# One layer of a hybrid decoder on one core: weight columns streamed in two interleaved halves, and segment sums kept in PSUM

## The chip, the cores and the metric

The kernel runs on one core of a Trainium2 chip. The metric is the device time of one execution in microseconds (us). Before the change the median of three runs is 2433.56 us (2433.44 to 2435.43).

## The reference, cut to what matters

Input is a float32 matrix of 256 tokens by 2048 features. The layer is an FFN, a two-branch mixer and a second FFN, each followed by a layer norm.

```
swiglu(h, w_in, w_out):  a, b = split(h @ w_in, 2);  return (silu(a) * b) @ w_out     # 2048 -> 2 x 5632 -> 2048
h = layer_norm(ALPHA*h + 0.5*swiglu(h, ffn1_w_in, ffn1_w_out))
q, k, v, qi, ki, wi, rx, rg, gates = split(h @ w_in)
y_attn = indexer-selected sparse attention(q, k, v, qi, ki, wi)
y_rnn  = gated linear recurrence(rx, rg)
merged = g_attn * (y_attn @ w_attn_branch) + g_rnn * (y_rnn @ w_rnn_branch)
h = layer_norm(ALPHA*h + merged @ w_out)
h = layer_norm(ALPHA*h + 0.5*swiglu(h, ffn2_w_in, ffn2_w_out))
```

## The kernel before, in words

**Products.** Every float32 operand is split into a high and a low part of the type fp32r: ScalarE rounds (`wh`, line 192), VectorE subtracts (`wl`, line 193). A product is then three matmuls, high by high, high by low and low by high. There are two kinds. In the *token-major* products the activations are the stationary operand (128 tokens at a time) and the weights stream past, 512 or 256 columns in one matmul; they all go through `three` (lines 553 to 556) and write 128 tokens by 512 columns of output. They are the two FFNs, the attention projections (`blockA`) and the product with `w_out`. In the others (`blockB`, `block3`) the weights are stationary and the activations stream; these are not touched by the change.

**Weights.** `Weights` walks a fixed list of pieces of 128 by 1024. A piece is loaded from HBM by SyncE's queue, split by ScalarE and VectorE four pieces ahead of TensorE, and consumed by `unit`. There are five buffers each of `wh` and `wl`.

**The FFN.** The 5632 hidden features are worked off in 22 blocks of 256 (a block holds 256 columns of each half of `w_in`). In most blocks three quarters of the sum over the 2048 features ("chunks") use a scheme with seven instead of eight 128x256 products for two-by-two tiles (forms `p1q3`, `p2`, `q5p7`, `q4p6`), with sums that VectorE forms beforehand (lines 165 to 172); the last quarter is plain ("c"). A block's result lies in two PSUM banks `c` and two banks `e`; `gate` (lines 842 to 871) joins them, applies the gate and transposes.

**The second product of the FFN** is spread over the blocks. The 22 blocks form six segments, `SEGS`, of 2, 4, 4, 4, 4 and 4 blocks. While a segment is worked off, the product of the segment before it with its rows of `w_out` runs as *fills* ("o" in a block's plan), for one 512-column stripe `nb` of the output after the other. Blocks 2 to 5 have two fills each, blocks 6 to 21 have four ("steady blocks" below): two at the start of the block, one after three forms, one after nine, and then three more forms. So each block from 2 on completes one stripe of one segment: two PSUM banks, one for each half of the tokens. `y_add` (line 689) then adds 0.5 times each bank to the running sum `Y[t][nb]` in SBUF; this is one VectorE instruction for each half. The last segment's product comes after the blocks (`out_product`).

**PSUM.** Eight banks: four under the tag `mm` (handed out in turn by `MM` to the `c` banks, to the fills, and to the products of the mixer), four under `bp`.

**Order.** TensorE, SyncE and GpSimd issue in the order in which the program is written. The instructions of ScalarE and VectorE are put in order by the scheduler of the language when the program is built.

Of the kernel before, what the change touches and what calls it, by code (L numbers as in the profile page):

```python
# [261 lines left out]
def tile_layer(ctx, tc, x_fm, x_tm, pos, f1a, f1o, wA, wki, wB, lru, wab, wrb, wo, f2a, f2o,  # L262
# [24 lines left out]
    def C(shape, s, dt=F32):  # L287
        return pool.tile(shape, dt, name=s)

    def MM():  # L290
        return psum.tile([P, 512], F32, name=name("mm"), tag="mm", bufs=4)

    def BP():
        return psum.tile([P, 512], F32, name=name("bp"), tag="bp", bufs=4)
# [255 lines left out]
            mmB(ps, x[k], W.unit(P), k == 0, k == len(x) - 1)  # L550
        return ps

    def three(ps, xh, xl, w, start, stop):
        T.matmul(ps, xh, w[0], start=start, stop=False)  # L554
        T.matmul(ps, xh, w[1], start=False, stop=False)  # L555
        T.matmul(ps, xl, w[0], start=False, stop=stop)  # L556

    def tokens(ps, x, t, w, start, stop):
        three(ps, x[:, 0, t * P:(t + 1) * P], x[:, 1, t * P:(t + 1) * P], w, start, stop)

    def eager(x, ps):

# [16 lines left out]
    def blockF(x, forms, plan, fill):  # L579

        c = e = None

        seen = set()
        last = {f: i for i, (f, k) in enumerate(plan)}
        top = max(last["c"], last.get("p2", 0)), max(last["c"], last.get("q4p6", 0))
        skip = 0
        if getattr(x, "halves", None):
            c = [MM(), MM()]  # L590
            eager(x, c)
            skip = 4
        for i, (form, k) in enumerate(plan):
            if i < skip:
                continue
            if form == "o":
                fill()
                continue
            if form == "c":
                if not c:  # L600
                    c = [MM(), MM()]
                    half = [c[0][:, :S], c[0][:, S:], c[1][:, :S]]
                for k in range(k, k + 2):
                    w = W.unit(512)
                    for t in range(2):
                        tokens(c[t], x[k], t, w, k == 0, k % 2 == 1 and i == top[t])
                continue
            if not e:
                e = [BP(), BP()]
                p1, p6, p7, q5 = e[0][:, :S], e[0][:, S:], e[1][:, :S], e[1][:, S:]  # L610
            start = form not in seen
            seen.add(form)
            stop = i == last[form]
            fs = [forms[2 * k + r] for r in range(2)]

            def xop(r, i, t):
                v = x[4 * k + 2 * r + i]
                return v[:, 0, t * P:(t + 1) * P], v[:, 1, t * P:(t + 1) * P]

            def sop(r, i):  # L620
                return tuple(v[:, i * P:(i + 1) * P] for v in fs[r])

            def run(ps, op, start, stop):
                for r in range(2):
                    three(ps, *op(r), W.unit(S), start and r == 0, stop and r == 1)

            if form == "p1q3":
                run(p1, lambda r: xop(r, 0, 0), start, False)
                run(half[1], lambda r: sop(r, 3), False, False)
            elif form == "p2":  # L630
                run(half[0], lambda r: xop(r, 1, 0), False, i == top[0])
            elif form == "q5p7":
                run(q5, lambda r: sop(r, 0), start, False)
                run(p7, lambda r: sop(r, 2), False, stop)
            else:
                run(half[2], lambda r: xop(r, 1, 1), False, i == top[1])
                run(p6, lambda r: sop(r, 1), False, stop)
        return c, e
# [202 lines left out]
    def ffn(x, forms, ln, plans):  # L841
        def gate(c, e, g, i, lag):

            z = W.fast_pool.tile([P, 4 * S], F32, name=name("z"), tag="z", bufs=Z_BUFS)
            z4 = z.rearrange("p (j c) -> p j c", j=4)
            a, b = z4[:, 0:4:2], z4[:, 1:4:2]
            if e:
                p1, p6, p7, q5 = e[0][:, :S], e[0][:, S:], e[1][:, :S], e[1][:, S:]
                A.activation(z4[:, 0], p1, AF.Copy)
                V.tensor_tensor(z4[:, 1], z4[:, 0], p6, op=OP.add)  # L850
                V.tensor_tensor(z4[:, 2], z4[:, 1], p7, op=OP.add)
                V.tensor_tensor(b, q5[:, None, :].to_broadcast([P, 2, S]), z4[:, 1:3], op=OP.subtract)
                for t in range(2):
                    zt = z[:, t * 512:(t + 1) * 512]
                    V.tensor_tensor(zt, zt, c[t], op=OP.add)  # L855
                A.activation(a, a, AF.Silu)
            else:
                for t in range(2):
                    A.activation(z4[:, 2 * t], c[t][:, :S], AF.Silu)
                    A.activation(z4[:, 2 * t + 1], c[t][:, S:], AF.Copy)  # L860
            V.tensor_tensor(a, a, b, op=OP.mult)
            for _ in range(lag):
                yield
            ps = BP()
            for k in range(2):
                for t in range(2):
                    T.transpose(ps[:, k * S + t * P:k * S + (t + 1) * P], z[:, t * 512 + k * P:t * 512 + (k + 1) * P], ident)  # L867
            for k in range(2):
                hl = UHL("g")
                split(hl, ps[:, k * S:(k + 1) * S])  # L870
                g[i + k] = hl

        g = [[None] * (2 * (b1 - b0)) for b0, b1 in SEGS]
        fills = iter(FILLS)
        open_ps = []

        def fill():
            s, nb, k0 = next(fills)
            if k0 == 0:
                open_ps[:] = MM(), MM()  # L880
            for k in (k0, k0 + 1):
                w = W.unit(512)
                for t in range(2):
                    tokens(open_ps[t], g[s][k], t, w, k == 0, k == len(g[s]) - 1)
            if k0 + 2 == len(g[s]):
                for t in range(2):
                    y_add(open_ps, nb, False, t)

        for s, (b0, b1) in enumerate(SEGS):
            for n in range(b0, b1):  # L890
                c, e = blockF(x, forms, plans[n], fill)
                task = gate(c, e, g[s], 2 * (n - b0), LAG_T[n == NBK - 1])
                next(task)
                bg.add("gate", task)
        new_stats()
        ln.prepare()
        if not ln.last:
            bg.add("main", later(consts(), W.last.ins))
        out_product(g[-1], ln)
# [306 lines left out]
def _layout(x, positions, ffn1_w_in, ffn1_w_out, ln1_g, ln1_b, w_in, conv_w, conv_b, lru_wa, lru_ba,  # L1206
# [5 lines left out]
        return np.ascontiguousarray(a)  # L1212

    def f_in(w):
        return c(w.reshape(NK, P, 2, NBK, 256).transpose(3, 1, 0, 2, 4)).reshape(NBK, P, NK * 512)

    def f_out(w):
        return c(w.reshape(NKF, P, 4, 512).transpose(2, 1, 0, 3)).reshape(4, P, NKF * 512)

    def a_blocks(w):  # L1220
        n = w.shape[1] // 512
        return c(w.reshape(NK, P, n, 512).transpose(2, 1, 0, 3)).reshape(n, P, NK * 512)

    def b_blocks(w):
        nk, n = w.shape[0] // P, w.shape[1] // P
# [52 lines left out]
```

## Time and profile before

| what | value |
|---|---|
| median of three runs | 2433.56 us |
| span of the profiled execution, and its own time | 2433.4 us |
| TensorE busy | 2400.1 us (99%) |
| VectorE busy | 2041.4 us (84%) |
| ScalarE busy | 1413.4 us (58%) |
| DMA, mean over the span | 190 GB/s |
| mean granted clock of TensorE | 0.996 of 2.4 GHz |

Read it so: TensorE has matmuls under way at nearly all times, but that says nothing of the rate at which they run. That has to be read from the distance between the starts of neighbouring matmuls. VectorE's 84% is a mean over stages: in the FFNs it is far higher than in the mixer. The first FFN takes about the first 695 us, the mixer lies between, and the second FFN begins shortly after 1700 us.

### The profile page before, as it was taken

The page shows a single profiled execution, that of the slowest core. Times are in us where ns is not written, and L with a number is a line of the kernel's source. Part 1 is how long each engine was busy: PE and PEld are TensorE (multiplying, and loading weights), DVE is VectorE, ACT ScalarE, POOL GpSimd, SP SyncE. Part 2 cuts the span into 40 slices and gives each one's busy share as a digit, 9 for nine tenths or more (in the row PEclk, how much of TensorE's full clock was granted, in tenths as well). Part 3 has the DMA queues.
Part 4 walks back from the last instruction along what each step waited for, and adds up shares of the span by engine and source line. Part 5 has one row for each costly group of instructions (what it writes and reads, how often), then busy time and mean ns, then how long its engine had stood idle before and what let it go on. Part 6 is the DMA issues. An engine that isn't in the chain of part 4 may idle for free.

```text
span 2433.4 us, 37546 instructions
## 1 busy us (share of the span) xinstructions
PE 2400.1 (99%) x14592; PEld 2117.5 (87%) x14592; DVE 2041.4 (84%) x2835; ACT 1413.4 (58%) x1931; POOL 25.9 (1%) x58
## 2 busy tenths in 40 slices
PE   8999999999999999999999999999999999999997
PEld 7888889888878788889999988887888888888885
DVE  8999999999987676555788875655999999999996
ACT  7555556656546455544688874444665555565562
POOL 0000000000000000000000000000000000000001
PEclk9999999999999999999999999999999999999998
DMA  8545555555456554455555565565655555555563
GB/s 291 187 176 188 208 208 208 205 187 205 183 165 216 166 164 147 152 186 184 181 185 188 181 197 184 188 186 181 209 206 195 203 195 187 186 188 218 208 212 113
DMA packets 112770, 463.41 MB, mean 190 GB/s; under 512 B 12720, under 2 KB 12720, under 8 KB 97488
## 3 DMA queue, kind: packets, MB, share of 16 engines
q1 hardware_dynamic: 110592, 454.61, 54.5%
q0 software_dynamic: 2000, 6.41, 1.0%
q8 instruction: 114, 1.87, 0.3%
q14 instruction: 64, 0.52, 0.1%
HBM read 458.87 MB, written 2.10 MB: 189 GB/s over the span
## 4 chain that ended last, share of the span: by engine, by line
PE 91%; issue 4%; DVE 3%; DMA 1%; ACT 1%; POOL 0%; SPq 0%; DVEq 0%; ACTq 0%; POOLq 0%
PE mm L554 16%; PE mm L556 16%; PE mm L555 16%; PE mm L544 11%; PE mm L545 5%; PE bp L556 4%; PE bp L555 4%; PE bp L554 4%; PE mm L1129 4%; PE mm L1130 4%; PE mm L1128 4%; DVE wl L193 2%; PE bp L867 1%; DMA raw<-f1a 0%; DVE ws L165 0%
## 5 line engine op out<-in xcount | busy, mean ns | idle before, releaser
L193 DVE TENSOR_TENSOR wl<-raw,wh 128x1024 fp32r<-128x1024 f32 (+3 forms) x630 | 753.1, 1203 | 290.2 <-ACT wh L192 289.0
L192 ACT ACTIVATE wh<-raw 128x1024 fp32r<-128x1024 f32 (+3 forms) x630 | 653.8, 1046 | 550.5 <-PE mm L556 290.6
L192 ACT ACTIVATE wh<-rf 128x1024 fp32r<-128x1024 f32 x354 | 321.0, 917 | 172.2 <-PE mm L556 138.4
L193 DVE TENSOR_TENSOR wl<-rf,wh 128x1024 fp32r<-128x1024 f32 x354 | 366.8, 1043 | 5.5 <-ACT wh L192 2.6
L554 PE MATMUL mm<-wh,g 128*128 128x512 f32 x704 | 282.2, 401 | 2.0 <-ACT g L679 2.0
L556 PE MATMUL mm<-wh,g 128*128 128x512 f32 x704 | 279.7, 397 | 1.3 <-DVE g L680 1.3
L555 PE MATMUL mm<-wl,g 128*128 128x512 f32 x704 | 279.0, 396 | 0.0
L554 PE MATMUL mm<-wh,hs 128*128 128x512 f32 (+1 forms) x728 | 265.4, 365 | 1.9 <-DVE z L855 1.9
L556 PE MATMUL mm<-wh,hs 128*128 128x512 f32 (+1 forms) x728 | 261.2, 359 | 1.1 <-DVE hs L745 1.1
L555 PE MATMUL mm<-wl,hs 128*128 128x512 f32 (+1 forms) x728 | 260.6, 358 | 0.0
L192 ACT ACTIVATE wh<-ws 128x1024 fp32r<-128x1024 f32 x118 | 125.3, 1062 | 163.8 <-issue 70.4
L556 PE MATMUL bp<-wh,sl 128*128 128x256 f32 x708 | 198.0, 280 | 0.0
L554 PE MATMUL bp<-wh,sh 128*128 128x256 f32 x708 | 197.6, 279 | 0.0
L555 PE MATMUL bp<-wl,sh 128*128 128x256 f32 x708 | 197.5, 279 | 0.0
L544 PE MATMUL mm<-hs,wh 128*128 128x512 f32 x528 | 190.1, 402 | 0.0
L1128 PE MATMUL mm<-hs,wh 128*128 128x256 f32 x640 | 179.8, 281 | 0.0
L1130 PE MATMUL mm<-hs,wl 128*128 128x256 f32 x640 | 179.8, 281 | 0.0
L1129 PE MATMUL mm<-hs,wh 128*128 128x256 f32 x640 | 179.8, 281 | 0.0
L554 PE MATMUL mm<-wh,xs 128*128 128x256 f32 (+1 forms) x464 | 158.5, 342 | 8.5 <-ACT wh L192 6.2
L556 PEld LDWEIGHTS mm<-wh,g 128*128 128x128 f32 x704 | 132.7, 189 | 34.6 <-DVE g L680 2.5
L193 DVE TENSOR_TENSOR wl<-ws,wh 128x1024 fp32r<-128x1024 f32 x118 | 144.5, 1224 | 19.8 <-ACT wh L192 19.8
L554 PEld LDWEIGHTS mm<-wh,hs 128*128 128x128 f32 x728 | 136.6, 188 | 28.0 <-issue 4.3
(255 smaller groups left out, 5347.8 us busy)
## 6 DMA issues: line engine op xcount, KB each, us to landing
raw<-wB SPq DMA_DIRECT2D x144, 512.0 KB, 3.8
rf<-f1a SPq DMA_DIRECT2D x60, 1024.0 KB, 4.8
rf<-f2a SPq DMA_DIRECT2D x58, 1024.0 KB, 5.0
raw<-f1o SPq DMA_DIRECT2D x88, 512.0 KB, 5.7
raw<-f2o SPq DMA_DIRECT2D x88, 512.0 KB, 5.9
raw<-wA SPq DMA_DIRECT2D x64, 512.0 KB, 3.6
raw<-f2a SPq DMA_DIRECT2D x60, 512.0 KB, 4.9
raw<-f1a SPq DMA_DIRECT2D x56, 512.0 KB, 5.8
```

The source lines that it names most:

```text
L192: nc.scalar.activation(hp, src, AF.Copy)
L193: self.last = nc.vector.tensor_tensor(lp, src, hp, op=OP.subtract)
L544: T.matmul(ps, w[0], x.rearrange("p a t -> p (a t)"), start=first, stop=False)
L545: T.matmul(ps[:, :S], w[1], x[:, 0], start=False, stop=last)
L554: T.matmul(ps, xh, w[0], start=start, stop=False)
L555: T.matmul(ps, xh, w[1], start=False, stop=False)
L556: T.matmul(ps, xl, w[0], start=False, stop=stop)
L867: T.transpose(ps[:, k * S + t * P:k * S + (t + 1) * P], z[:, t * 512 + k * P:t * 512 + (k + 1) * P], ident)
L1128: T.matmul(ps[:, :S], w[0], x[:, 0], start=first, stop=False)
L1129: T.matmul(ps[:, :S], w[0], x[:, 1], start=False, stop=False)
L1130: T.matmul(ps[:, :S], w[1], x[:, 0], start=False, stop=last)
```

## The change

It has two parts. In the first, `three` hands its two weight operands to the matmul through another view: of each 256 columns as they lie in SBUF, the matmul now takes column 0, column 128, column 1, column 129 and so on, that is, two runs of addresses 512 bytes apart, in alternation. The weights are laid out in HBM on the host so that the outputs stand in the same order as before. Loads, splits and sums see tiles of the same shape.

In the second, the PSUM tag `mm` becomes two tags of two banks each: `CB` (still named `mm`) for the `c` banks, `OB` (`ob`) for the fills; the other users take one and the other in turn. For segments 1 to 4 of each FFN (the steady blocks) the sum is no longer added by VectorE. Before a stripe's first fill, ScalarE writes 2 times `Y[t][nb]` into the stripe's two banks (`seed`, line 891 of the new file); the fills accumulate onto this; at the end ScalarE writes 0.5 times the bank back to `Y[t][nb]` (line 904). The seeds of the next stripe are issued directly behind that. Segment 0 and the last segment are added by VectorE as before.

```
     def CB():  return psum.tile([P, 512], F32, name=name("mm"), tag="mm", bufs=2)
     def OB():  return psum.tile([P, 512], F32, name=name("ob"), tag="ob", bufs=2)
     def MM():
-        return psum.tile([P, 512], F32, name=name("mm"), tag="mm", bufs=4)
+        turn[0] ^= 1
+        return CB() if turn[0] else OB()
...
-    def three(ps, xh, xl, w, start, stop):
-        T.matmul(ps, xh, w[0], start=start, stop=False)
-        T.matmul(ps, xh, w[1], start=False, stop=False)
-        T.matmul(ps, xl, w[0], start=False, stop=stop)
+    def three(ps, xh, xl, w, start, stop, seeded=False):
+        h, l = (v.rearrange("p (a h c) -> p a c h", h=2, c=P) for v in w)
+        T.matmul(ps, xh, h, start=start, stop=False, skip_group_check=seeded)
+        T.matmul(ps, xh, l, start=False, stop=False, skip_group_check=seeded)
+        T.matmul(ps, xl, h, start=False, stop=stop, skip_group_check=seeded)
...
-            c = [MM(), MM()]
+            c = [CB(), CB()]
...
+        def seed():
+            s, nb, _ = fills[0]
+            open_ps[:] = OB(), OB()
+            for t in range(2 if s else 0):
+                A.activation(open_ps[t], Y[t][nb], AF.Copy, scale=2.0)
         def fill():
-            s, nb, k0 = next(fills)
-            if k0 == 0:
-                open_ps[:] = MM(), MM()
+            if not open_ps:
+                seed()
+            s, nb, k0 = fills.popleft()
...
-                    tokens(open_ps[t], g[s][k], t, w, k == 0, k == len(g[s]) - 1)
+                    tokens(open_ps[t], g[s][k], t, w, not s and k == 0, k == len(g[s]) - 1, bool(s))
             if k0 + 2 == len(g[s]):
                 for t in range(2):
-                    y_add(open_ps, nb, False, t)
+                    if s:
+                        A.activation(Y[t][nb], open_ps[t], AF.Copy, scale=0.5)
+                    else:
+                        y_add(open_ps, nb, False, t)
+                if fills:
+                    seed()
...
     def f_in(w):
-        return c(w.reshape(NK, P, 2, NBK, 256).transpose(3, 1, 0, 2, 4)).reshape(NBK, P, NK * 512)
+        return c(w.reshape(NK, P, 2, NBK, P, 2).transpose(3, 1, 0, 2, 5, 4)).reshape(NBK, P, NK * 512)
```

(`f_out` and `a_blocks` are laid out in the same way.)

TensorE issues the same matmuls in the same order. Two places show what moves. The first is ScalarE's list at the end of a steady block, where the last fill of a stripe completes (`rf`, `raw`, `ws` are weight pieces and sums of them, `z` the gate's tile, `ob` the fill's bank). Before:

```order
L192 ACTIVATE wh134_2679<-raw134_2605 128x1024
L192 ACTIVATE wh135_2697<-raw135_2623 128x1024
L192 ACTIVATE wh136_2709<-raw136_2642 128x1024
L192 ACTIVATE wh137_2725<-rf137_2661 128x1024
L849 ACTIVATE z131_2743<-bp126_2482 128x256
```

And of the changed kernel:

```order
L192 ACTIVATE wh134_2685<-raw134_2611 128x1024
L904 ACTIVATE y49_381<-ob121_2373 128x512
L891 ACTIVATE ob131_2703<-y51_403 128x512
L904 ACTIVATE y50_383<-ob122_2374 128x512
L192 ACTIVATE wh135_2707<-raw135_2629 128x1024
L891 ACTIVATE ob132_2704<-y52_405 128x512
L192 ACTIVATE wh136_2719<-raw136_2648 128x1024
```

Four instructions now stand between the splits of the pieces 134 and 136, one split (135) among them. The pieces 134 and 135 are those of the next block's first two fills.

The second place is TensorE's list where block 1 of the first FFN ends and the plain part of block 2 begins (`xs` is the split input, `sh` and `sl` the combined inputs of the forms), with the engines whose results an instruction waits for. Before:

```order
L556 MATMUL bp56_445<-wh19_566,sl48_378 128x256
L554 MATMUL mm62_657<-wh20_583,xs9_120 128x512 [waits Activation_49]
L555 MATMUL mm62_657<-wl20_584,xs9_120 128x512 [waits DVE_49]
L556 MATMUL mm62_657<-wh20_583,xs9_120 128x512
L554 MATMUL mm63_658<-wh20_583,xs9_120 128x512 [waits PE_49]
```

And of the changed kernel:

```order
L566 MATMUL bp56_445<-wh19_566,sl48_378 128x256
L564 MATMUL mm62_657<-wh20_583,xs9_120 128x512 [waits DVE_49,PE_49,Activation_49]
L565 MATMUL mm62_657<-wl20_584,xs9_120 128x512
L566 MATMUL mm62_657<-wh20_583,xs9_120 128x512
L564 MATMUL mm63_658<-wh20_583,xs9_120 128x512 [waits DVE_49,PE_49]
```

The rows are the same matmuls, but each of the two banks is now waited for: with two `c` banks instead of four in turn, block 2 takes over the banks of block 1, whose gate (on VectorE) has just begun to read them.

## Rows read from the trace of the kernel before

**Rows 1.** The page's busy times over the whole span.

```profile
PE 2400.1 (99%) x14592; PEld 2117.5 (87%) x14592; DVE 2041.4 (84%) x2835; ACT 1413.4 (58%) x1931; POOL 25.9 (1%) x58
```

**Rows 2.** Stretches: us, busy of PE, PEld, DVE, ACT, POOL; clock, DMA share, GB/s.

```profile
60.00:160.00 100.00, 99.66 (x628) 88.80 (x627) 98.12 (x120) 57.14 (x70) 0.00 (x0) 1.00 0.54 193
300.00:440.00 140.00, 140.00 (x886) 125.19 (x885) 135.41 (x162) 82.47 (x98) 0.00 (x0) 1.00 0.52 192
690.00:760.00 70.00, 68.61 (x301) 54.68 (x302) 57.66 (x143) 39.56 (x75) 5.51 (x10) 0.98 0.61 191
760.00:840.00 80.00, 79.89 (x383) 63.81 (x383) 55.71 (x125) 37.36 (x58) 0.00 (x0) 1.00 0.57 172
```

**Rows 3.** Timeline of TensorE near the end: start us, duration us, instruction.

```profile
2409.16 0.40 PE L556 MATMUL mm<-wh,g 128*128 128x512 f32 x1
...
2413.83 0.40 PE L555 MATMUL mm<-wl,g 128*128 128x512 f32 x1
```

**Rows 4.** Two stretches of 2 us, columns as in rows 2.

```profile
692.00:694.00 2.00, 2.00 (x7) 1.52 (x6) 1.42 (x3) 0.00 (x0) 0.00 (x0) 0.50 0.36 145
...
2410.00:2412.00 2.00, 2.00 (x11) 1.59 (x10) 0.00 (x0) 0.00 (x0) 0.00 (x0) 1.00 0.00 0
```

**Rows 5.** Timeline of TensorE within the first of them.

```profile
691.84 0.63 PE L554 MATMUL mm<-wh,g 128*128 128x512 f32 x1
...
693.97 0.63 PE L556 MATMUL mm<-wh,g 128*128 128x512 f32 x1
```

**Rows 6.** Timeline of TensorE in the forms of a steady block.

```profile
400.15 0.28 PE L554 MATMUL mm<-wh,sh 128*128 128x256 f32 x1
...
401.90 0.28 PE L554 MATMUL bp<-wh,sh 128*128 128x256 f32 x1
```

**Rows 7.** Groups of matmuls by form: line, operands, shape, count, busy us, mean ns.

```profile
L554 PE MATMUL mm<-wh,g 128*128 128x512 f32 x704 | 282.2, 401 | 2.0 <-ACT g L679 2.0
...
L554 PE MATMUL mm<-wh,hs 128*128 128x512 f32 x496 | 200.1, 403 | 1.9 <-DVE z L855 1.9
...
L554 PE MATMUL bp<-wh,sh 128*128 128x256 f32 x708 | 197.6, 279 | 0.0
...
L554 PE MATMUL mm<-wh,xs 128*128 128x512 f32 x224 | 91.1, 406 | 8.5 <-ACT wh L192 6.2 <-DVE z L855 2.3
...
L554 PE MATMUL mm<-wh,mg 128*128 128x512 f32 x128 | 50.6, 396 | 0.0
...
L554 PE MATMUL bp<-wh,hs 128*128 128x256 f32 x116 | 32.5, 280 | 0.0
```

**Rows 8.** Timeline of VectorE: additions to Y in two steady blocks.

```profile
324.12 1.28 DVE L689 SCALAR_TENSOR_TENSOR y<-mm,y 128x512 f32<-128x512 f32 x2
325.32 2.35 DVE L193 TENSOR_TENSOR wl<-raw,wh 128x1024 fp32r<-128x1024 f32 x2
...
420.06 1.28 DVE L689 SCALAR_TENSOR_TENSOR y<-mm,y 128x512 f32<-128x512 f32 x2
```

**Rows 9.** What VectorE waited for, 160 to 640 us: total us, times, longest.

```profile
DVE wl L193 <- ACT wh L192: 10.6, 17, 1.1
DVE z L861 <- ACT z L856: 3.7, 14, 0.3
```

**Rows 10.** Timeline of ScalarE where a steady block's last fill ends.

```profile
355.82 2.02 ACT L192 ACTIVATE wh<-raw 128x1024 fp32r<-128x1024 f32 x2 [1.73 <-PE mm L556]
357.89 1.07 ACT L192 ACTIVATE wh<-rf 128x1024 fp32r<-128x1024 f32 x1
```

**Rows 11.** ScalarE's groups by form that copy 128x512.

```profile
L961 ACT ACTIVATE stg<-mm 128x512 f32<-128x512 f32 x16 | 9.6, 599 | 13.5 <-PE mm L556 13.5
...
L521 ACT ACTIVATE y<-y 128x512 f32<-128x512 f32 x8 | 4.5, 616 | 0.0
```

**Rows 12.** Timeline, all engines, where block 2 of the first FFN begins.

```profile
61.01 0.39 PE L554 MATMUL mm<-wh,xs 128*128 128x512 f32 x1
...
62.66 1.29 DVE L855 TENSOR_TENSOR z<-z,mm 128x512 f32<-128x512 f32 x2
```

More of the change, by code (lines that the diff above doesn't have):

```diff
@@ L288, in C, with CB, OB @@
         return pool.tile(shape, dt, name=s)
+    def CB():
+        return psum.tile([P, 512], F32, name=name("mm"), tag="mm", bufs=2)
+    def OB():
+        return psum.tile([P, 512], F32, name=name("ob"), tag="ob", bufs=2)
+    turn = [0]
     def MM():
-        return psum.tile([P, 512], F32, name=name("mm"), tag="mm", bufs=4)
+        turn[0] ^= 1
+        return CB() if turn[0] else OB()
     def BP():
@@ L551, in blockB, with tokens @@
         return ps
-    def three(ps, xh, xl, w, start, stop):
-        T.matmul(ps, xh, w[0], start=start, stop=False)
-        T.matmul(ps, xh, w[1], start=False, stop=False)
-        T.matmul(ps, xl, w[0], start=False, stop=stop)
-    def tokens(ps, x, t, w, start, stop):
-        three(ps, x[:, 0, t * P:(t + 1) * P], x[:, 1, t * P:(t + 1) * P], w, start, stop)
+    def three(ps, xh, xl, w, start, stop, seeded=False):
[3 more added lines that the diff above has]
+        T.matmul(ps, xl, h, start=False, stop=stop, skip_group_check=seeded)
+    def tokens(ps, x, t, w, start, stop, seeded=False):
+        three(ps, x[:, 0, t * P:(t + 1) * P], x[:, 1, t * P:(t + 1) * P], w, start, stop, seeded)
     def eager(x, ps):
@@ L600, in blockF @@
                 if not c:
-                    c = [MM(), MM()]
+                    c = [CB(), CB()]
                     half = [c[0][:, :S], c[0][:, S:], c[1][:, :S]]
@@ L873, in ffn @@
         g = [[None] * (2 * (b1 - b0)) for b0, b1 in SEGS]
-        fills = iter(FILLS)
+        fills = deque(FILLS)
         open_ps = []
+        def seed():
[3 more added lines that the diff above has]
+                A.activation(open_ps[t], Y[t][nb], AF.Copy, scale=2.0)
         def fill():
-            s, nb, k0 = next(fills)
-            if k0 == 0:
-                open_ps[:] = MM(), MM()
+            if not open_ps:
+                seed()
+            s, nb, k0 = fills.popleft()
             for k in (k0, k0 + 1):
@@ L1214, in f_in @@
     def f_in(w):
-        return c(w.reshape(NK, P, 2, NBK, 256).transpose(3, 1, 0, 2, 4)).reshape(NBK, P, NK * 512)
+        return c(w.reshape(NK, P, 2, NBK, P, 2).transpose(3, 1, 0, 2, 5, 4)).reshape(NBK, P, NK * 512)
     def f_out(w):
-        return c(w.reshape(NKF, P, 4, 512).transpose(2, 1, 0, 3)).reshape(4, P, NKF * 512)
+        return c(w.reshape(NKF, P, 4, 2, P, 2).transpose(2, 1, 0, 3, 5, 4)).reshape(4, P, NKF * 512)
     def a_blocks(w):
         n = w.shape[1] // 512
-        return c(w.reshape(NK, P, n, 512).transpose(2, 1, 0, 3)).reshape(n, P, NK * 512)
+        return c(w.reshape(NK, P, n, 2, P, 2).transpose(2, 1, 0, 3, 5, 4)).reshape(n, P, NK * 512)
     def b_blocks(w):
```

## The prediction

> **What bounds the kernel now.** I read the page's busy times first, then the stretches, then the distance between matmuls, then the waits. TensorE is busy 2400 of 2433 us [rows 1], so nothing but a faster or shorter stream of matmuls, or the end of a wait, can shorten the kernel. In a steady stretch of an FFN TensorE is busy 140.00 us of 140, but VectorE 135.41, that is 97% [rows 2]: two engines are near their limit there, and a gain of TensorE runs into VectorE after 3%. In the attention projections (690 to 840 us) VectorE is busy 113 of 150 us [rows 2], and TensorE alone counts.
>
> How fast does TensorE run? From 2409.16 to 2413.83 us lie 20 distances between starts: 4.67 us / 20 = 233.5 ns for 512 columns [rows 3]. In the forms, 15 distances from 400.15 to 401.90 us give 116.7 ns for 256 [rows 6]. Both are 0.456 ns a column, so the cost goes with the columns and not with the instruction. Behind two waits for the gate near 690 us the granted clock fell to 0.50, which is 1.2 of 2.4 GHz [rows 4]; there five distances from 691.84 to 693.97 us give 426 ns for 512 columns [rows 5], 0.832 ns each, exactly one column in a clock. At 2.4 GHz the same would be 213 ns. So the array could take a column in each clock, and at full clock some 20 ns of 233.5 are lost to something that does not keep up. It is not contention: in the stretch 2410 to 2412 us VectorE, ScalarE and the DMA stand still [rows 4], and the distance is the same 233.5 ns. What is left is the supply of the moving columns or the writing of the sums, at a rate of its own that only shows at full clock. Only the first of these is touched by the change.
>
> **The read in two streams.** It changes nothing in number or size of the matmuls, only the order of addresses. No row shows such a read, so I bound it. Best: the loss goes wholly, 213.4 ns for 512 and 106.7 for 256. Worst shown pace: one column in each clock of 1.2 GHz, 426 ns for 512 [rows 5]. I take the best end, for one reason from the rows: a single stream shows no loss when it advances at 1.2 columns per ns [rows 5], and in the interleaved read each of the two streams advances at 2.4 / 2 = 1.2. If the loss lies in how fast one run of addresses can be followed, both streams stay below it. If it lies in the total of bytes or in the writes, nothing changes (a rival).
>
> The matmuls concerned, from the code with its counts in the rows: 512 columns, 3 x (704 + 496 + 224 + 128) = 4656; 256 columns, 3 x 1652 = 4956 (six groups a line, from 708 to 116) [rows 7]. TensorE's own saving would be 4656 x 20.1 + 4956 x 10.0 ns = 94 + 50 = 144 us. Not all of it comes through.
>
> *Steady blocks, 16 in each FFN.* Their additions to Y come at 324.12 us and, three blocks later, at 420.06: 31.98 us a block [rows 8]. TensorE's part is 72 x 233.5 + 126 x 116.7 ns = 31.5 us plus 0.4 for four transposes, which fits. With the better read it is 72 x 213.4 + 126 x 106.7 = 28.8 plus 0.4 = 29.2 us. VectorE's part is 31.98 x 135.41/140 = 30.93 us [rows 2]. The second part of the change takes two additions out of each block; from 324.12 to 325.32 us they hold the engine for 1.20 us [rows 8]. That leaves 29.73, more than TensorE's 29.2, so VectorE becomes the limit. It also waits now: 14.3 us in the 480 us to 640 us [rows 9], 0.95 us a block. Most of that is slack, since ScalarE itself waits for buffers that TensorE still reads; the 0.25 for the gate is not. I take 30.1 us a block, between 29.7 and 30.7: 32 x 1.88 = 60 us saved.
>
> *What ScalarE gets.* Four instructions of 128x512 in each steady block. A write from SBUF into PSUM is not shown; the nearest rows are 599 ns for PSUM to SBUF and 616 for SBUF to SBUF [rows 11], so 2.4 us a block on an engine that is busy 82.47 of 140 us [rows 2]. Its load rises from 59 to some 70%. The first of them waits for the last fill, and behind it stand the splits for the next block. That is harmless in the amount that I see: at 355.82 us, where a last fill ends, ScalarE begins the two splits that its order now mixes with the four [rows 10]. With 0.6 us for each of the three and 1.05 for the split between, the second seed is written 0.6 x 4 + 1.05 = 3.5 us after the fill. TensorE has three forms to do in that time, 30 matmuls of 106.7 ns = 3.2 us, and needs the second bank only three matmuls of 512 (0.64 us) later. So the seeds arrive just in time: nothing, and up to 0.5 us a block (16 us in all) if ScalarE is late. The split that comes 1.8 us later than before belongs to a fill that TensorE reaches some 6 us after.
>
> *Fewer banks for `c`.* Three block beginnings in each FFN (blocks 1, 2 and 4) now take over the banks of the block just ended. Before, the fills at the start of blocks 3 and 5 did so, which the trace shows as waits for the gate's line 855 of at most 1.9 us each (within the 1.9 and 2.3 us of [rows 7]). The price of such a wait: at 61.01 us TensorE begins block 2, and the gate of block 1 reads its banks from 62.66 to 63.95 us [rows 12], so TensorE and all matmuls behind would wait about 2.4 us. Six times 2 us less the old 4 is 8; but around there VectorE is busy 98.12 of 100 us [rows 2] and catches up meanwhile. I take 4, between 0 and 10.
>
> *The rest.* Blocks 2 to 5 keep their additions and are VectorE's already (98%): nothing. Block 0 and 1 of the second FFN, 192 matmuls of 512: 192 x 20 ns = 4. The first FFN's start hangs on loads and splits: 0. The two closing products of the FFNs, 192 each: 8. The projections, 8 blocks of 16 x 2 x 3 = 768, with VectorE at 75%: 15. The product with `w_out`, 384 [rows 7]: 8. The DMA share is 0.52 to 0.61 in these stretches [rows 2] and hides the faster loads. SyncE's and GpSimd's lists are the same as before.
>
> Sum: 60 + 4 + 8 + 15 + 8 - 4 = 91 us. The profiled span is 2433.4 us, within 0.2 us of the median, so nothing has to be added: 2433.4 - 91 = 2342, and 2343 with half a microsecond a block at a few late seeds. With the steady block between 29.7 and 30.9 us and the waits at their bounds the likeliest case lies between 2325 and 2375.
>
> **The rivals.**
> *The supply gets slower.* Alternating between addresses 512 bytes apart could cost more than following one run. It decides as soon as a 512-column matmul takes more than 233.5 ns, since TensorE has no slack in the FFNs (140.00 of 140 us). At the pace of one column in each 1.2 GHz clock [rows 5] the price is 4656 x 192.5 + 4956 x 96.3 ns = 1373 us: 3807 us. Against it: a stream's own pace would stay at one that the rows show to be free of loss. For it: no row shows any read by TensorE that is not contiguous, and a loss that goes with columns could as well come from jumps in the addresses, of which there would be more. The Trainium skill (SBUF — State Buffer, "Door 1: The DMA port swizzle") speaks for this rival: SBUF is read in lines of 16 bytes, and an access that crosses to a new line pays unless at least two in a row hit the same. By that rule a contiguous float32 read has four hits a line and should lose nothing, yet the trace shows 20 ns lost; an interleaved read has one hit a line and would lose. The trace of before thus does not bear the rule out in its first half and cannot show its second.
>
> *The read changes nothing.* If the loss lies in bytes per ns or in the writes into PSUM, TensorE stays the bound. Then VectorE's 1.2 us a block are idle time of an engine that is not the limit, and the added waits cost 0 to 8 us: 2433 to 2441, taken as 2436.
>
> *Half of the loss goes.* At 223.5 and 111.7 ns the steady block is 16.1 + 14.1 + 0.4 = 30.6 us by TensorE, the rest saves half: 32 x 1.4 + 17 - 4 = 58 us, 2375 us. The same time would come out if the seeds were late by 1 us in each of the 32 blocks.
>
> **How the numbers follow.** A difference under 0.2% (5 us) can't be told from none. The forecast gets 0.66; half of the gain or late seeds (2375 to 2428) 0.13; no change of the read 0.08, of which 0.06 falls within 5 us and 0.02 above; the slower supply 0.13. So faster 0.79, the same 0.06, slower 0.15. The range that leaves out no more than two in ten reaches from 2318 (steady block at VectorE's floor and all waits at nothing, with a little for the banks) to 2436, the case without a faster read.
>
> **What would show it.** In the changed profile the distance between starts of 512-column matmuls in `three` should be near 213 ns and that of 256 near 107 wherever TensorE does not wait, while the untouched `blockB` and `block3` keep 0.456 ns a column. Additions to Y on ScalarE should come every 30 us in the steady blocks, with VectorE at 98% or more there, and TensorE should now wait for VectorE's `wl`. Waits for line 865 (the old 855) should stand at the beginnings of blocks 1, 2 and 4. The prediction is wrong if the distance stays at 233 ns or grows, if it falls and the block still takes over 31 us, or if TensorE waits for the seeds by more than 0.5 us a block.

## The result and the profile after

The changed kernel takes 2451.16 us (median of 4 runs, 2446.72 to 2452.09) against 2433.50 us for the kernel before on the same chip: a ratio of 1.0064, 95% interval 1.0052 to 1.0077. It is slower by 18 us, where 91 us less were forecast. The profiled execution has a span of 2449.2 us against 2433.4, so the traces differ by 16 us, nearly as much as the medians.

The page's busy times, after (in each entry: busy us, share of the span, instructions):

```profile
PE 2315.0 (95%) x14592; PEld 2105.0 (86%) x14592; DVE 2016.9 (82%) x2771; ACT 1472.5 (60%) x2059; POOL 25.9 (1%) x58
```

Against [rows 1] TensorE works 85 us less for the same 14592 matmuls. But it now stands idle 134 us, where it had stood idle 33. So the matmuls did become faster, and more than the gain went into waiting.

First the pace. TensorE's timeline in a steady block, after, for 512 columns (`three`'s lines are 564 to 566 now) and for 256:

```profile
399.15 0.38 PE L564 MATMUL ob<-wh,g 128*128 128x512 f32 x1
...
401.53 0.38 PE L566 MATMUL ob<-wh,g 128*128 128x512 f32 x1
...
402.41 0.28 PE L564 MATMUL bp<-wh,sh 128*128 128x256 f32 x1
...
404.98 0.28 PE L566 MATMUL bp<-wh,sl 128*128 128x256 f32 x1
```

Between the first two rows lie 11 distances between starts, 2.38 us / 11 = 216.4 ns (233.5 in [rows 3]); between the last two lie 23, 111.7 ns (116.7 in [rows 6]). The read does nearly what was forecast.

Then the stretches, the same as in [rows 2], with the same columns:

```profile
60.00:160.00 100.00, 86.31 (x525) 78.90 (x526) 83.14 (x102) 48.23 (x58) 0.00 (x0) 0.91 0.43 153
300.00:440.00 140.00, 132.89 (x893) 123.10 (x892) 132.38 (x153) 91.97 (x117) 0.00 (x0) 1.00 0.54 202
...
760.00:840.00 80.00, 78.40 (x404) 67.73 (x404) 59.30 (x122) 46.52 (x78) 0.00 (x0) 1.00 0.65 205
```

In the first blocks (60 to 160 us) TensorE now works 86 of 100 us, with a granted clock of 0.91, and gets through 525 matmuls where it had done 628. In the steady stretch it works 133 of 140 us, and 893 matmuls stand against 886: nothing is gained there. Only the projections gain (404 matmuls against 383, with TensorE busy 78.40 of 80 us).

Which waits? The view of waits, after: total us, times, longest.

```profile
PE mm L564 <- DVE z L865: 93.9, 37, 9.0
```

Line 865 is the gate's addition of `c` on VectorE, the old line 855, for which TensorE waited 4.2 us in all before. It now costs 94 us, in 37 waits. TensorE's timeline at the beginnings of blocks 1, 2 and 4 of the first FFN, before the plain part of two steady blocks (it follows on their first two fills), and at the closing products of the first FFN (start, duration, instruction, idle time before it and its releaser):

```profile
34.41 0.48 PE L564 MATMUL mm<-wh,xs 128*128 128x512 f32 x1 [2.34 <-ACT z L870]
...
56.52 0.28 PE L566 MATMUL bp<-wh,sl 128*128 128x256 f32 x1
...
64.32 0.77 PE L564 MATMUL mm<-wh,xs 128*128 128x512 f32 x1 [7.52 <-DVE z L865]
...
125.80 0.77 PE L564 MATMUL mm<-wh,xs 128*128 128x512 f32 x1 [9.04 <-DVE z L865]
...
348.10 0.45 PE L564 MATMUL mm<-wh,xs 128*128 128x512 f32 x1 [1.78 <-DVE z L865]
...
380.15 0.45 PE L564 MATMUL mm<-wh,xs 128*128 128x512 f32 x1 [1.76 <-DVE z L865]
...
699.16 0.77 PE L564 MATMUL mm<-wh,g 128*128 128x512 f32 x1 [5.19 <-DVE z L865]
```

At 34, 64 and 126 us the waits are 2.3, 7.5 and 9.0 us long (the first is for ScalarE, which reads the banks of block 0, and is not among the 94 us); the last form of block 1 had started at 56.52 us and block 2's first matmul follows at 64.32. In the second FFN there is one such wait, of 9.0 us at block 4. The closing products of both FFNs wait too, 5.2 and 3.9 us. And in every steady block there is one of 1.8 us (2.7 at the first of each FFN); the kernel before had one of 1.9 us at the first of each FFN (171.17 us) and none at the others. The two steady blocks lie 32.05 us apart (31.98 before, 30.1 forecast).

By stage, from the start of the same matmul in both traces: a last one of the first FFN's closing products stands at 747.83 us instead of 726.50 (+21), the first one with `w_out` at 1617.92 instead of 1607.85 (+10), the first one of the second FFN at 1702.64 instead of 1699.07 (+4), and one of its last at 2433.05 instead of 2417.56 (+15). So the first FFN loses 21 us, the projections give back 11 and the product with `w_out` 6.5, and the second FFN loses 12.

### The profile page after: what moved, and what is told of

The parts are those of the page before. It is cut to its first block, busy times and chain, and to the rows that moved or that the text cites. A ratio compares the mean times of both kernels' runs of the same rounds, so it can differ in the third digit from the quotient of the medians.

```text
span 2449.2 us, 37523 instructions
## 1 busy us (share of the span) xinstructions
PE 2315.0 (95%) x14592; PEld 2105.0 (86%) x14592; DVE 2016.9 (82%) x2771; ACT 1472.5 (60%) x2059; POOL 25.9 (1%) x58
## 4 chain that ended last, share of the span: by engine, by line
PE 72%; DVE 16%; issue 7%; ACT 4%; DMA 1%; POOL 0%; ACTq 0%; DVEq 0%; SPq 0%; POOLq 0%
DVE wl L193 8%; PE mm L564 8%; PE mm L566 7%; PE mm L565 7%; PE mm L553 5%; PE ob L553 5%; PE ob L564 4%; PE ob L566 4%; PE ob L565 4%; PE bp L565 3%; PE bp L566 3%; PE bp L564 3%; PE mm L554 3%; PE ob L554 3%; ACT wh L192 2%
## 5 line engine op out<-in xcount | busy, mean ns | idle before, releaser
L564 PE MATMUL ob<-wh,g 128*128 128x512 f32 x640 | 247.2, 386 | 1.0 <-ACT g L689 1.0
L564 PE MATMUL mm<-wh,hs 128*128 128x512 f32 (+1 forms) x600 | 208.1, 347 | 40.0 <-DVE z L865 38.7
L566 PE MATMUL ob<-wh,g 128*128 128x512 f32 x640 | 244.0, 381 | 0.6 <-DVE g L690 0.6
L565 PE MATMUL ob<-wl,g 128*128 128x512 f32 x640 | 243.8, 381 | 0.0
L564 PE MATMUL mm<-wh,xs 128*128 128x256 f32 (+1 forms) x464 | 155.4, 335 | 55.9 <-DVE z L865 46.1
L566 PE MATMUL mm<-wh,hs 128*128 128x512 f32 (+1 forms) x600 | 205.6, 343 | 1.7 <-DVE hs L755 1.4
L565 PE MATMUL mm<-wl,hs 128*128 128x512 f32 (+1 forms) x600 | 205.3, 342 | 0.0
L564 PEld LDWEIGHTS mm<-wh,hs 128*128 128x128 f32 x600 | 114.9, 192 | 58.4 <-ACT wh L192 32.6
L565 PE MATMUL mm<-wl,xs 128*128 128x256 f32 (+1 forms) x464 | 153.4, 331 | 1.6 <-DVE wl L193 1.6
L566 PE MATMUL mm<-wh,xs 128*128 128x256 f32 (+1 forms) x464 | 152.9, 330 | 0.0
L564 PEld LDWEIGHTS mm<-wh,xs 128*128 128x128 f32 x464 | 89.6, 193 | 70.4 <-ACT wh L192 40.7
L165 DVE TENSOR_TENSOR ws<-rf 128x1024 f32<-128x1024 f32 x118 | 144.2, 1222 | 4.1 <-DMA rf<-f2a 1.1
L565 PEld LDWEIGHTS bp<-wl,sh 128*128 128x128 f32 x708 | 135.8, 192 | 3.6 <-DVE wl L193 2.4
```

The source lines that it names most:

```text
L165: v.tensor_tensor(t, b[:, 0:4:3], b[:, 1:2].to_broadcast([P, 2, 2, 256]), op=OP.add)
L564: T.matmul(ps, xh, h, start=start, stop=False, skip_group_check=seeded)
L565: T.matmul(ps, xh, l, start=False, stop=False, skip_group_check=seeded)
L566: T.matmul(ps, xl, h, start=False, stop=stop, skip_group_check=seeded)
```

## The experiments

Four theories stood against each other at first. *A*: the loss comes from the gate. With two banks for `c` TensorE takes over banks that VectorE has not read yet, and VectorE's list now puts the gate's additions later. *B*: ScalarE's four new instructions in a block delay the splits, and with them the matmuls. *C*: the interleaved read slows somebody else. *D*, from the prediction: VectorE catches up during the waits, so they cost little. Later came *E*: the banks only hurt because TensorE has become faster.

**The parts one by one.** The kernel before with the read alone:

```
+        h, l = (v.rearrange("p (a h c) -> p a c h", h=2, c=P) for v in w)
...      # f_in, f_out, a_blocks laid out as in the change
```

> Only the interleaved read (with its weight layout) on the kernel before; four banks in turn, additions to Y on VectorE. Theory A (the loss comes from the fewer c banks: TensorE waits for the gate's additions, which stand behind splits in VectorE's list): no waits for the gate over 2 us at the starts of blocks 1, 2 and 4; the projections and the product with w_out keep their 20 us, the FFNs gain a little up to VectorE's 30.9 us a block: 2380 to 2410 us. Theory B (ScalarE's four instructions a block delay the splits): nearly the same, 2375 to 2400. Theory C (the faster read takes something from the other engines, so that an FFN block stays at 32 us whatever else is done): steady blocks at 32.0 us, 2410 to 2415.

2385.58 us, ratio 0.9796 [0.978, 0.9813]: the read alone is worth 49 us. VectorE and ScalarE are busy 2036 and 1410 us (2041 and 1413 before), and the steady block is shorter, so C is out. One steady block of it (columns as in rows 2), and TensorE and VectorE where the plain part of the next begins:

```profile
392.00:423.40 31.40, 30.28 (x202) 28.00 (x203) 30.95 (x38) 18.77 (x22) 0.00 (x0) 1.00 0.55 201
...
423.40 0.45 PE L555 MATMUL mm<-wh,xs 128*128 128x512 f32 x1 [1.11 <-ACT wh L192]
```

```profile
422.57 1.28 DVE L856 TENSOR_TENSOR z<-z,mm 128x512 f32<-128x512 f32 x2
```

The block is 31.40 us, with VectorE busy 30.95 of them: without the seeds VectorE becomes the bound, as the prediction had said. The wait is put down to a split on ScalarE. One does end just before the matmul (423.38 us), but it belongs to a later piece; the split of the piece needed here was done by 416.9 us. What else ended just then is the first of the gate's two additions, begun at 422.57 us, 0.83 us before the matmul. This distance is the same within 0.02 us in the changed kernel and in the six others of this section whose steady blocks wait at this place, whichever engine the profile names and wherever ScalarE's split ends. So the gate stands in the way even with four banks in turn, once TensorE is faster.

The changed kernel with the contiguous read, that is banks and seeds:

```
-        h, l = (v.rearrange("p (a h c) -> p a c h", h=2, c=P) for v in w)
+        h, l = w
...      # layouts as before the change
```

> Only the banks and the seeds, with the contiguous read of before. Theory A: the early waits for the gate appear (shorter than in the changed kernel, since TensorE arrives later: 2 to 6 us each at blocks 1, 2 and 4), steady blocks with little or no wait: 2440 to 2455 us. Theory B: steady blocks grow by the time the splits come late, 32.3 us or more, 2445 to 2460. Theory C: 2433 to 2440.

2515.28 us, ratio 1.033 [1.0315, 1.0345]. The direction was that of A and B, but the time is above both ranges. VectorE has two additions less in each block, and yet a steady block takes 33.35 us, as the gate's additions show:

```profile
390.76 1.28 DVE L865 TENSOR_TENSOR z<-z,mm 128x512 f32<-128x512 f32 x2
...
424.11 1.28 DVE L865 TENSOR_TENSOR z<-z,mm 128x512 f32<-128x512 f32 x2
```

So the seeds themselves, or what came along with them, cost time even with the contiguous read.

The read with the split of the banks, VectorE still adding to Y:

```
-            c = [MM(), MM()]
+            c = [CB(), CB()]
-                open_ps[:] = MM(), MM()
+                open_ps[:] = OB(), OB()
```

> The interleaved read and the split of the banks (two for c, two for the fills), but no seeds: additions to Y stay on VectorE. Theory A: the early waits of 2, 7 and 9 us in each FFN are back and with them some 35 us against the read alone; steady blocks wait for the gate as in the changed kernel: 2430 to 2450 us. Theory B: as the read alone, 2375 to 2405. Theory C: about 2415 plus the early waits, 2440.

2428.78 us, ratio 0.9976 [0.9965, 0.9988]: the banks cost 43 us on top of the read. The steady block is 31.41 us, as with the read alone, so all of it lies outside the steady blocks: most at the first blocks, and 8 us in waits of 4.8 and 3.5 us before the closing products. The stretch 60 to 160 us of this kernel, its waits there, and what VectorE and ScalarE do behind the first of them:

```profile
60.00:160.00 100.00, 86.42 (x531) 79.15 (x532) 84.40 (x104) 49.51 (x59) 0.00 (x0) 0.93 0.44 153
...
64.20 0.77 PE L564 MATMUL mm<-wh,xs 128*128 128x512 f32 x1 [7.52 <-DVE z L865]
...
125.97 0.77 PE L564 MATMUL mm<-wh,xs 128*128 128x512 f32 x1 [9.04 <-DVE z L865]
...
69.83 1.23 DVE L193 TENSOR_TENSOR wl<-raw,wh 128x1024 fp32r<-128x1024 f32 x1 [3.72 <-ACT wh L192]
...
68.73 1.07 ACT L192 ACTIVATE wh<-raw 128x1024 fp32r<-128x1024 f32 x1 [3.35 <-PE mm L566]
```

The same stretch and the same two waits as in the changed kernel, without any seed. VectorE is busy 84 of 100 us: if it caught up while TensorE waits, as D says, it would be busy to the full. Its splits run some pieces ahead, and then need buffers that TensorE must first free: behind the wait VectorE stands idle for 3.7 us, for a split on ScalarE that itself waits for TensorE.

The split of the banks on the kernel before, with the contiguous read:

> Only the split of the banks, contiguous read, additions to Y on VectorE. With the read, the same split cost 43 us (2428.8 against 2385.6). Theory A (the cost is the waits at the beginnings of blocks 1, 2 and 4, which hang on VectorE's list and not on TensorE's pace): about the same, 30 to 45 us, 2465 to 2480, steady blocks at 31.98. Theory E (the cost comes only from TensorE being faster): 2433 to 2445.

2476.85 us, ratio 1.0173 [1.0156, 1.019]: 41 us, the same price as with the interleaved read. E is out. The steady block stays at 31.98 us. TensorE's timeline at the beginnings of blocks 2 and 4 and at the closing products of the first FFN, its waits for the gate in all, and the stretch behind the first wait (columns as in rows 2):

```profile
65.08 0.77 PE L563 MATMUL mm<-wh,xs 128*128 128x512 f32 x1 [7.22 <-DVE z L864]
...
128.82 0.76 PE L563 MATMUL mm<-wh,xs 128*128 128x512 f32 x1 [7.81 <-DVE z L864]
...
704.17 0.76 PE L563 MATMUL mm<-wh,g 128*128 128x512 f32 x1 [4.60 <-DVE z L864]
...
PE mm L563 <- DVE z L864: 33.3, 9, 7.8
PE mm L563 <- ACT z L869: 2.2, 2, 1.4
...
65.60:69.90 4.30, 4.30 (x11) 3.30 (x10) 1.23 (x2) 0.63 (x1) 0.00 (x0) 0.50 0.00 0
```

Here is the working of the 41 us: waits of 35.5 us against 4.2 before are 31. Five make up most of them: 7.2 and 7.8 us at blocks 2 and 4 of the first FFN, 7.8 at block 4 of the second, and 4.6 and 3.2 before the closing products. Behind each of these the granted clock stands at 0.50, which is 1.2 GHz, for 2 to 6 us (4.3 us in the row shown), and a matmul of 512 columns takes 426 instead of 233.5 ns. Some 68 matmuls follow one another at that pace in this trace and some 33 in the trace of before: 35 x 0.19 = 7 us. That makes 38 of 41.

**The order of the gate.** What of the seeds slows the steady block? VectorE's timeline there, and TensorE's first matmul of the plain part, before:

```profile
330.59 0.69 DVE L852 TENSOR_TENSOR z<-bp,z 128x512 f32<-128x512 f32 x1
331.19 0.69 DVE L172 TENSOR_TENSOR rf<-rf 128x512 f32<-128x512 f32 x1
331.79 1.28 DVE L855 TENSOR_TENSOR z<-z,mm 128x512 f32<-128x512 f32 x2
332.98 1.23 DVE L193 TENSOR_TENSOR wl<-ws,wh 128x1024 fp32r<-128x1024 f32 x1
...
332.69 0.40 PE L554 MATMUL mm<-wh,xs 128*128 128x512 f32 x1
```

And after:

```profile
345.54 0.69 DVE L862 TENSOR_TENSOR z<-bp,z 128x512 f32<-128x512 f32 x1
346.14 1.22 DVE L193 TENSOR_TENSOR wl<-ws,wh 128x1024 fp32r<-128x1024 f32 x1
347.27 1.28 DVE L865 TENSOR_TENSOR z<-z,mm 128x512 f32<-128x512 f32 x2
```

The split `wl<-ws,wh` stood behind the gate's additions and now stands ahead of them. Nobody wrote that: the list is made by a scheduler. In the traces of the kernels with the additions to Y on VectorE (before, the read alone, the banks with either read) the split stands behind, in the two with seeds ahead; what in the scheduler moves it was not tried. It is 1.13 us long to the next start. Before, the plain part of the next block began at 332.69 us, 0.90 us after the first addition; where TensorE has to wait for it, the distance is 0.83. So the margin was under 0.1 us, and can't carry 1.1. That refines A, and the next kernel tests it: the changed kernel with the later splits held behind the gate.

```
-                    V.tensor_tensor(zt, zt, c[t], op=OP.add)
+                    W.after = V.tensor_tensor(zt, zt, c[t], op=OP.add).ins
...      # where a piece is split:
+                with self.tc.issue_after(self.after):
+                    self.split_one(step)
```

> The changed kernel with one thing different: VectorE's splits of pieces that are asked for after a block's gate stand behind the gate's additions, so c comes free about 2.4 us of VectorE work earlier. Theory A: the 1.8 us waits at the steady blocks go and the early ones get 1 to 2 us shorter; steady block 30.3 to 31.2 us: 2395 to 2425 us. Theory B: the wait for the gate is only where a late VectorE shows; steady block stays 32.0 and the wait moves to the splits (wl): 2443 to 2452. Theory C: the same as B.

2390.68 us, ratio 0.9821 [0.9805, 0.9838]: the order of VectorE's list was worth 60 us, more than A's range said. ScalarE has the same four instructions at the same place of its list in each block, so B is out. A steady block, TensorE where the plain part of the next begins, and VectorE's list around the gate (lines are some ten higher in this kernel):

```profile
398.04:428.62 30.58, 30.28 (x202) 28.00 (x203) 30.12 (x36) 20.50 (x26) 0.00 (x0) 1.00 0.58 207
...
428.62 0.45 PE L574 MATMUL mm<-wh,xs 128*128 128x512 f32 x1 [0.30 <-DVE z L875]
```

```profile
396.48 0.69 DVE L872 TENSOR_TENSOR z<-bp,z 128x512 f32<-128x512 f32 x1
397.21 1.29 DVE L875 TENSOR_TENSOR z<-z,mm 128x512 f32<-128x512 f32 x2
```

The gate follows directly on line 872, the wait is 0.30 instead of 1.78 us, and the block 30.58 instead of 32.05. Beside the split `wl<-ws,wh`, three instructions of 0.6 us for half a piece went behind the gate too, so what the one split costs by itself is not shown. 32 blocks by 1.47 us are 47 of the 60. Another 9 lie in the long waits: 7.5, 9.0 and 9.0 us at the first blocks shrink to 5.0, 6.5 and 6.5, and 5.2 and 3.9 before the closing products to 4.5 and 3.2.

The same order without the banks and seeds, on the kernel with the read alone:

> The interleaved read alone, with the order of VectorE's list as in the kernel with the gate first; no seeds, four banks in turn. Theory A: the 1.1 to 1.4 us waits for the gate at the steady blocks go, but VectorE is busy 98% there already, so little comes of it: 31.0 to 31.4 us a block, 2372 to 2386 us. Theory D': the order alone, not VectorE's load, was the limit, and the seeds are worth nothing: steady block 30.6, 2360.

2385.14 us, ratio 0.9789 [0.9773, 0.9806]: no difference from the read alone (2385.58). Its steady block is 31.32 us, and VectorE is busy 31.14 of them (388.00 to 419.32 us): with all its additions it is the bound there, and the order of its list doesn't matter. So the order gains nothing where VectorE is full, and 60 us where the seeds leave it room. Banks and order without seeds were not run, so what the seeds alone are worth is not shown.

And on the kernel with the contiguous read, banks and seeds:

> Banks and seeds with the contiguous read, and the gate's additions first in VectorE's list. Without that order the steady block took 33.34 us. Theory A (the order made it slow): steady block back at 31.9 to 32.1 us, TensorE's own time, the early waits some 2 us shorter each: 2455 to 2472 us. Theory B (ScalarE's four instructions made it slow): 33.0 or more, 2500 or more.

2463.64 us, ratio 1.0121 [1.0106, 1.0136]: 52 us less than without the order (2515.28). Two gates of its steady blocks, and a stretch of some three blocks:

```profile
376.12 1.28 DVE L875 TENSOR_TENSOR z<-z,mm 128x512 f32<-128x512 f32 x2
...
408.12 1.28 DVE L875 TENSOR_TENSOR z<-z,mm 128x512 f32<-128x512 f32 x2
...
312.00:409.00 97.00, 97.00 (x612) 86.95 (x611) 91.63 (x108) 62.33 (x79) 0.00 (x0) 1.00 0.54 196
```

32.00 us a block, what the kernel before takes, with TensorE busy 97.00 of 97 us: with the contiguous read TensorE is the bound again, and the extra 1.4 us a block of the kernel with banks and seeds were the order's doing, not that of ScalarE's four instructions.

**The first blocks.** The last step on the changed kernel, beside the order: block 1 takes the `OB` banks for its `c`, which no fill uses then, and block 4 begins with fills as the blocks behind it do.

```
-                    c = [CB(), CB()]
+                    c = [CB(), CB()] if fresh else [OB(), OB()]
...
-    [block_plan(2, 2, 0), block_plan(3, 2)] * 2
+    [block_plan(2, 2, 0), block_plan(3, 2), block_plan(2, 2), block_plan(3, 2)]
```

> The kernel with the gate's additions first, and besides: block 1 of each FFN takes the banks of the fills for its c, and block 4 begins with its two fills instead of its c. Theory A (what is left over the floor is the waits for c at the beginnings of blocks 1, 2 and 4, 14 us in each FFN and some time at the lower clock behind them): 2390.7 - 2 x (12 to 17) = 2357 to 2368 us. Theory D (those first blocks are VectorE's anyway, which catches up in the waits): 2380 to 2390.

2370.36 us, ratio 0.973 [0.9716, 0.9745]: 65 us below the kernel before and 81 below the changed one. The same first stretch and the waits in all:

```profile
60.00:160.00 100.00, 96.14 (x635) 88.28 (x634) 99.43 (x122) 58.08 (x73) 0.00 (x0) 1.00 0.55 195
...
PE mm L574 <- DVE z L879: 20.3, 34, 4.5
```

VectorE is busy 99.43 of 100 us instead of 83.14, the clock stays at 1.00, and 635 matmuls are done instead of 525. It beats the read alone with the same order by 15 us, which is what banks, seeds and the two changes at the first blocks are worth together. The time is 2 us above A's range, and waits for the gate of 20 us are left, 4.5 and 3.2 us of them before the closing products.

**The read by itself.** Four kernels, one run each, change nothing but the number of streams and their distance, with the weights laid out in HBM to match. Two streams 32 bytes apart (`h=2, c=8`) and 256 bytes apart (`h=2, c=64`):

> Read alone, two streams in turn, 32 bytes apart (within 16 columns). If two runs of addresses in alternation are enough whatever their distance, 216 ns for 512 columns, 2385 us. If the distance counts (four streams at 256 bytes took 284 ns, a step of 8 bytes 453 ns), 233 ns or more and a time over 2433 us.

> Read alone, two streams in turn, 256 bytes apart. If the number of streams decides, 216 ns for 512 columns and 2385 us as at 512 bytes; if the distance of 256 bytes was what made four streams slow, 284 ns and 2780 us.

2385.62 and 2385.94 us, and 2385.58 with 512 bytes apart: of these three distances none matters. Four streams 256 bytes apart (`h=4, c=64`), and one stream that takes every second column (`"p (a c e) -> p a e c", c=128, e=2`):

> As the read alone, but four streams 256 bytes apart in turn. If alternating between runs of addresses is what lets the supply keep up, 512 columns take 216 ns or less again and the time is 2380 to 2390 us. If it was the distance of 512 bytes, or two streams exactly, the distance between starts goes back to 233 ns or more and the time to 2433 or more.

> As the read alone, but a single stream that takes every second column of a 256-column run and then the others (steps of 8 bytes). If two runs of addresses in alternation are needed, 233 ns or more for 512 columns and 2433 us or more. If any read that leaves the plain run of neighbours does it (the loss lies in neighbouring addresses), 216 ns and 2380 to 2390.

2782.11 and 3991.61 us. The distance between starts is 216 ns for 512 columns with two streams 32 or 256 bytes apart. TensorE's timeline of the four streams (five distances between the rows, 282 ns):

```profile
419.93 0.45 PE L555 MATMUL mm<-wh,g 128*128 128x512 f32 x1
...
421.34 0.45 PE L557 MATMUL mm<-wh,g 128*128 128x512 f32 x1
```

And the one with a step of 8 bytes (nine distances, 453 ns):

```profile
619.75 0.65 PE L557 MATMUL mm<-wh,xs 128*128 128x512 f32 x1
...
623.83 0.65 PE L557 MATMUL mm<-wh,xs 128*128 128x512 f32 x1
```

Two streams are faster than one (233.5 ns) and than four (282 ns); three, or four at another distance, were not run. The prediction's reason, that each stream must advance more slowly, would have let four streams pass without loss; it gave nearly the right number for two, but it isn't the mechanism, so that number was in part luck. Nor is the rule it weighed against it. By the Trainium skill (SBUF — State Buffer, "Door 1: The DMA port swizzle") the lines have 16 bytes, and two hits on a line suffice for full speed; the step of 8 bytes has two hits on each line and is the slowest at 453 ns, while two alternating streams never hit the same line twice running and are the fastest. The runs here contradict the rule for this operand, and what does set the pace stays open.

The medians in one table (contiguous and interleaved read side by side, us):

| | contiguous | interleaved |
|---|---|---|
| nothing else | 2433.5 | 2385.6 |
| banks split | 2476.9 | 2428.8 |
| banks and seeds | 2515.3 | 2451.2 (the change) |
| banks and seeds, gate first | 2463.6 | 2390.7 |
| and the first blocks mended | – | 2370.4 |

## Why the prediction was wrong

*The read.* Right in direction and nearly in size: 216.4 ns was forecast as 213.4, 111.7 as 106.7. The projections and the product with `w_out` gained 11 and 6.5 of the 15 and 8 us forecast. The rival of a slower supply did not come.

*Fewer banks for `c`: the first step that failed.* It was priced at 4 us, bounds 0 to 10; it costs 41 to 43. Three things were wrong in it. It took the row at 61.01 us [rows 12] for the beginning of block 2, but that row is the block's second plain piece. TensorE's timeline of before, some microseconds earlier:

```profile
55.99 0.28 PE L556 MATMUL bp<-wh,sl 128*128 128x256 f32 x1
56.11 0.40 PE L554 MATMUL mm<-wh,xs 128*128 128x512 f32 x1
```

The last form ends the old block and block 2 begins at 56.11 us; the gate frees the first bank at 62.66 + 0.6 = 63.3 us. That is a wait of 7.2 us and not 2.4, to be read from the trace of before; the banks alone then showed 7.22. The second is "VectorE catches up meanwhile": the kernel with read and banks has VectorE at 84 of 100 us in that stretch, because the splits need buffers from the TensorE that waits. The third is the list of places, six block beginnings at 2 us each. With the banks alone three of them wait 7 to 8 us, the two blocks 1 wait 1.4 and 0.8 us, and block 2 of the second FFN does not wait; the closing products, where the prediction counted no wait, wait 4.6 and 3.2 us. Nor do the old waits of 1.9 us stand at the fills of blocks 3 and 5: they stand before the plain part of block 6 (171.17 and 1862.43 us). The low clock behind each long wait was left out too, though [rows 4] showed it.

*The steady block: the second step that failed.* Forecast 30.1 us, measured 32.05, and 30.58 once the order is mended. The 60 us that it was to save came to nothing. The sum of the two engines' work was nearly right: with the order mended TensorE is busy 30.28 us a block and VectorE 30.12 (29.2 and 29.73 forecast). What it took as given was the place of the gate in VectorE's list. The waits of 1.9 us in [rows 7] showed that the gate was late at the first steady block already, and at the others the margin was under 0.1 us. The order of the changed kernel, which is fixed when the program is built, already had the split ahead of the gate. The prediction read ScalarE's and TensorE's lists only. That the order of VectorE's list costs the 60 us is shown by holding the splits behind the gate, and that it costs 52 with the contiguous read by the two kernels with that one.

*The seeds.* Right: no wait of TensorE for a seed stands in the trace. ScalarE's timeline after a last fill:

```profile
337.18 0.60 ACT L904 ACTIVATE y<-ob 128x512 f32<-128x512 f32 x1 [0.73 <-PE ob L566]
337.81 0.61 ACT L891 ACTIVATE ob<-y 128x512 f32<-128x512 f32 x1
...
339.77 0.59 ACT L891 ACTIVATE ob<-y 128x512 f32<-128x512 f32 x1
```

A write from SBUF into PSUM takes 0.59 to 0.61 us (0.6 taken from [rows 11]), and the second seed is done 3.2 us after the first copy began (3.5 forecast). ScalarE's load went from 59 to 66% (70 forecast).

*The rivals.* None was what happened. The one on the slower side was about the read; the mechanism that decided, the gate holding the banks in every block, was only a term of a few microseconds in the forecast. The chance of 0.15 for slower stood on the wrong mechanism.

*What it would have taken.* With the waits read rightly (three of 7 to 8 us, two of 3 to 5, the short ones, and some 7 us of low clock) the term would have been about 40 us, and with the order's 1.5 us in each of 32 blocks another 47: 2343 + 36 + 47 = 2426, beside the 2451 measured. The remaining 25 are of the size that stays even with both mended, 2370 against 2343; there 20 us of waits for the gate are left. The matmuls, 3 and 5 ns longer than forecast, make up to 4656 x 3.0 + 4956 x 5.0 ns = 39 us of TensorE's time, part of which lies beside VectorE's work. How the rest divides between the two was not tried.

## What to carry to other kernels

When buffers are split or taken in a fixed role, find for each the last reader of the old content and the first writer of the new one in the trace, and make sure that the row taken as the first writer really is the first: the wait is their difference, and it comes again wherever a buffer changes hands in that way. Count every such place, also those behind the loop. When instructions are taken from a list that a scheduler orders, look through that engine's whole new list around the instruction on which the bound engine waits; a margin of 0.1 us does not survive a neighbour of 1.1 us. A wait on the bound engine isn't made up for by the other engines when their work needs buffers that the waiting engine must free.

## What the runs showed of the hardware

- The pace of TensorE in these matmuls depends on how the moving columns lie: 233.5 ns for 512 from one contiguous run, 216 from two runs in alternation (32, 256 or 512 bytes apart), 282 from four, 453 with a step of 8 bytes. At the lower clock the contiguous run shows no loss (426 ns).
- After waits of 7 to 9 us, and of 4.6 us at 704 us with the banks alone, the granted clock was 0.50 for 2 to 6 us. The length of the wait alone does not settle it: in the kernel before the clock was 0.50 from 172.8 to 175.8 us, behind a wait of 1.93 us, while in the changed kernel it stayed at 1.00 from 187.9 to 190.0 us, behind one of 2.72 us, and from 348.1 to 350.1 us, behind one of 1.78 us.
- The recorded releaser of a wait can be wrong where several semaphores are waited for: with the read alone the 1.1 us at each steady block are put down to ScalarE's split, while the matmul follows the start of the gate's addition by the same 0.83 us as in the kernels where the gate is named.
